# A fused encoder layer on one core: a reordered attention pipeline, more columns in the pair stage, and two half columns begun early

## The chip, the cores and the metric

The kernel runs on one core of one Trainium2 chip. The metric is the device time of one execution in microseconds, the median of several runs. A core has a matrix engine (PE, with its weight loads shown as PEld), a vector engine (DVE), a scalar engine (ACT), a general engine (POOL) and a queue engine (SP) that issues most transfers. Each engine works through its own instructions strictly in program order; semaphores tie the engines together.

## The reference

One layer of a streaming encoder, for 512 prompt tokens and 8 streams of 16 new tokens (640 rows together), with 2048 channels:

```
z = x @ w_in                  # q, k, v, forget and gate of attention; q, k, v, decay, beta and gate
                              # of the delta rule; two merge gates of 2048 columns each
A: 8 heads of forgetting attention (causal; the streams attend to 512 cached rows), * silu(gate) @ w_out_fox
B: 8 heads of the gated delta rule, convolution of width 4, in chunks,             * silu(gate) @ w_out_gdn
h  = (sigmoid(mA) * A + sigmoid(mB) * B) @ w_out
x1 = LayerNorm(2^0.25 * x + h)
y  = x1 + sigmoid(x1 @ w_pl_gate) * RMSNorm(p @ w_pl_proj)
```

Outputs are y, the new keys and values, log forgets, convolution tails and delta-rule states.

## The kernel before

**Columns and slots.** Activations lie transposed, 128 channels by 640 rows per tile. A *column* is 128 output channels. Every float32 operand is split into a high and a low part, and a product takes three matmuls. A *plain column* (`column`, with `mm6` at L396 and L397) has 16 *slots*; each does six matmuls of 320 rows, three for each half of the rows. A *pair* (`pair`, L474) computes two columns at once by a scheme of seven products of half size: 7 x 8 x 3 = 168 matmuls of 320 rows in place of 192. A *half pair* has half as many. The weights come as tiles of 1024 columns, and `w_piece` (L329, L332, L335, L342) splits them into pieces of 512: ACT copies the high part and DVE subtracts it for the low part; in the *accumulated* form ACT writes the negated high part and a transfer from POOL's queue adds the weights to it. A plain column takes 4 pieces, a pair 14 and four sums on DVE (`w_sum`, L319). At most five pieces are ahead. Some sums of weights are computed on POOL and kept in memory (`weight_sums`, L295).

**Stages.** First the *front*: two plain columns, four value columns (`wide`), then pairs: 8 for the gates, 2 for values, 11 for merge columns, 4 for queries and keys of the heads in `APART`. Then the *attention stage* (`phase_fox`): plain columns for the queries and keys of heads 1, 4 and 7, with three merge columns and the two columns of the embedding projection. Then the *delta-rule stage* (`phase_gdn`): three plain columns per head and as many merge columns behind head h as `FILL[h]` says; then two merge columns, `PLAIN` = 4 plain output columns of attention and four half pairs. Last the *tail*: the output columns of the delta rule, the pairs of w_out, and the gate.

**Order.** It is written out by a planner while the program is built. `tick` is called once per slot; each *lane* holds generators (attention, its decode part, outputs, convolution, block inverses, and so on) that issue some instructions and yield a number of slots to wait. The planner keeps a model of when each engine is done; a lane that yields a negative number goes on when the modelled finish less 1.5 us has come. The lanes on TensorE are looked at in every second slot (`every` = 2). `until` turns slots without dense matmuls until a condition holds; TensorE then has only what the lanes issue.

**Attention.** `fox_all` goes through 8 heads with four query blocks each. At each block `fox_step` moves a pipeline on: transposes of the block before last (L726), weights of the last one (`softmax2`, L655 and L656), the product with the values (L742) and the gate (L743); then `scores` of the new block (L388 to L390, L754, L759 to L650). `fox_dec` does the streams' part: scores against the cache (L773), softmax, and the product with cached values (L813). Cache tiles of the next head (4 of keys, 4 of values, 512 KB each) are loaded when those of this head are used. The first evacuation of the projection (`e_evac`) waits until the last decode is done.

**Delta rule.** Head by head a chain of generators: convolution, transposes and norms (`gdn`), block inverses (`gdn_blocks`, L1004 and L1006, 31 steps on DVE), merge, chunks, output (`gdn_out`, transposes at L1117). The half pairs need sums and splits of the attention outputs (`form_sums`, L1657; `form_splits`), and start only when head 7's inverses are done. The tail's first output column needs the last head's output in the last slot of each of its two groups.

Of the kernel before, what the change touches and what calls it, by code (L numbers as in the profile page):

```python
# [52 lines left out]
class Kernel:  # L53
# [19 lines left out]
    def __init__(self, tc, ins, outs):  # L73
        self.clock, self.busy, self.wrote, self.paced = 0.0, [0.0, 0.0, 0.0], {}, False
        self.tc, self.nc, self.i, self.o = tc, tc.nc, ins, outs
        self.lanes, self.every = [], 2
        self.banks, self.read, self.nbanks = [], {}, 3
        self.now = 0
# [119 lines left out]
    def plan(self):  # L198
# [55 lines left out]
        self.SUMMED = n - 48  # L254
# [144 lines left out]
    def column(self, cols=1, each=None, groups=((0, 16),), after=None, base=None, done=None):  # L399
# [7 lines left out]
        for n0, n1 in groups:  # L407
            ps = [tuple(self.gps(x.stop - x.start) for x in self.cut) for _ in range(cols)]
# [234 lines left out]
    def softmax1(self, xs, n):  # L643
# [3 lines left out]
        nm = self.zt([P, 1], "nm", 6)  # L647
        nc.vector.reduce_max(out=nm, in_=xs[:, 0:n], axis=AX.X, negate=True)
        sm = self.zt([P, 1], "sm", 6)
# [9 lines left out]
    def fox_in(self, h, q):  # L659

        nc = self.nc
        if h == 0:
            self.load_bias(0)
# [19 lines left out]

    def fox_all(self):


        flow = [None] * 4
        for h in range(H):
            while h not in self.heads or self.heads[h][2] > self.now or min(self.outdone, self.decdone) < h - 2:
                if any(flow):  # L690
                    self.fox_step(flow)
                yield 2
# [8 lines left out]
            for i in range(4):  # L701
                self.fox_step(flow)
                flow[0] = h, i, self.scores(h, i, q, k, parts)
# [14 lines left out]
    def fox_step(self, flow):  # L718

        nc = self.nc  # L720
        spread = weigh = None
        if flow[1]:
            h, i, (xs, _) = flow[1]
# [7 lines left out]
        if flow[0]:  # L731
            h, i, (xs, sm) = flow[0]
            self.softmax2(xs, P * (i + 1), sm)
            weigh = flow[0]
        if flow[2]:
            h, i, pT = flow[2]
            if i == 0:
                self.og = self.zt([P, T], "og", 2)
            vn, sl = self.vn[h], slice(i * P, (i + 1) * P)
            ops = self.sps()  # L740
            for kb in range(i + 1):
                nc.tensor.matmul(ops[:, 0:P], vn[:, kb, :], pT[:, kb * P:(kb + 1) * P], start=(kb == 0), stop=(kb == i))  # L742
            nc.vector.tensor_tensor(out=self.og[:, sl], in0=ops[:, 0:P], in1=self.sg[h][:, sl], op=ALU.mult)  # L743
            if i == 3:
                self.outs["gens"].append(self.fox_out(h, self.sg[h], self.og))
        flow[:] = None, weigh, spread, None

    def scores(self, h, i, q, k, parts):
# [9 lines left out]
        xs = self.zt([P, NPT], "xs", 3)  # L758
# [5 lines left out]
    def fox_dec(self, h, q, k):  # L764
# [12 lines left out]
        xd = self.zt([P, T], "xd")  # L777
# [12 lines left out]
        yield -2  # L790
        pt = self.dps()
# [10 lines left out]
        yield 4  # L802
# [418 lines left out]
    def run(self, ctx):  # L1221
# [18 lines left out]
        self.qkd = {(h, i): dr([P, T], F32, name=f"qkd{h}{i}") for h in (0, *self.APART) for i in range(2)}  # L1240
# [7 lines left out]
        self.outs, self.decs = self.lane(), self.lane()  # L1248
# [4 lines left out]
        with tc.manual_schedule():  # L1253
# [5 lines left out]
            with tc.tile_pool(name="ps2g", bufs=4, space=bass.MemoryType.PSUM) as self.ps2, \  # L1259
                    tc.tile_pool(name="cs2", bufs=1) as c2, tc.tile_pool(name="zg", bufs=1) as self.zp:  # L1260
                self.cvst = c2.tile([P, 24, 24], F32, name="cvst")
                nc.sync.dma_start(out=self.cvst, in_=self.i["conv"])
                self.nbanks = 4
                self.phase_gdn(conv, work)
            with tc.tile_pool(name="ps2b", bufs=4, space=bass.MemoryType.PSUM) as self.ps2, \
                    tc.tile_pool(name="zb", bufs=1) as self.zp:
                self.tail()
# [16 lines left out]
    def front(self, work):  # L1284
# [179 lines left out]
        def weights():  # L1464
# [3 lines left out]
            yield from self.weight_sums([t[:, x:x + 256] for t in ws for x in (0, 256)], slice(0, 12), (6, 4, 2))  # L1468
# [33 lines left out]
    def phase_fox(self, work):  # L1502
# [6 lines left out]
        self.heads, self.sg = {}, {}  # L1509
# [4 lines left out]
        ws = self.zt([P, 1024], "ws")  # L1514
        self.sums["gens"].append(self.weight_sums([ws[:, x:x + 256] for x in range(0, 1024, 256)], slice(12, 13),
                                                  (9, 7, 5, 20)))
        for h in range(H):
            qk = []
            if h in self.BETWEEN:
                self.mcol("eacc")  # L1520
            for c in range(2):
                stored = (h, c) in self.qkd
                if not stored:
                    acc = self.column()[0]
                self.until(lambda: min(self.qkdone) >= h - 2)
                x = self.zt([P, T], "qk"[c], 2)
                qk.append(x)
                if stored:
                    nc.sync.dma_start(out=x, in_=self.qkd[h, c])
                    continue  # L1530
                for hf in range(2):
                    sl = slice(hf * HALF, (hf + 1) * HALF)
                    if c == 0:
                        nc.scalar.mul(x[:, sl], acc[hf], FOX_SCALE)
                    else:
                        nc.scalar.copy(out=x[:, sl], in_=acc[hf])
                if c:
                    nc.sync.dma_start(out=self.o["fk"][h], in_=x)
            self.heads[h] = *qk, self.now + (9 if stored else 1)
        for _ in range(2 - len(self.BETWEEN)):  # L1540
            self.mcol("eacc")

        op, pr = [], []
        for k in range(2):
            if k == 0:
                self.until(lambda: not self.sums["gens"])
            pr.append(self.zt([P, 1024], "ws", 1, "pr")[:, 0:T] if k == 0 else self.zt([P, T], "pr"))
            nc.sync.dma_start(out=pr[k], in_=self.i["pT"][k])

        def after(s):  # L1550
            if s in (12, 14):
# [11 lines left out]
        nc.sync.dma_start(out=self.sqd, in_=self.eacc)  # L1563

# [10 lines left out]
    def phase_gdn(self, conv, work):  # L1575
# [76 lines left out]
        def form_sums(k, step):  # L1652

            a, b = fr[2 * k], fr[2 * k + 1]
            for o, x, y, op in ((b[:, xb], b[:, xb], a[:, xb], ALU.subtract), (a[:, xb], a[:, xb], a[:, xa], ALU.subtract),
                                (a[:, xa], b[:, xb], a[:, xa], ALU.add), (b[:, xa], b[:, xa], a[:, xa], ALU.subtract)):
                nc.vector.tensor_tensor(out=o, in0=x, in1=y, op=op)  # L1657
# [101 lines left out]
        store()  # L1759
        self.until(lambda: self.gdone == 7)  # L1760
# [15 lines left out]
    def e_evac(self, n, ps):  # L1776

        nc = self.nc
        if n == 0:
# [3 lines left out]
            tiles = [self.zt([P, 1024], *x, "e")[:, 0:T] for x in (("kc", 4), ("kc", 4), ("ws", 1), *[("vc", 4)] * 4)]  # L1783
# [59 lines left out]
    def tail(self):  # L1843
# [94 lines left out]
        for u in range(8):  # L1938
# [27 lines left out]
            self.column(groups=((0, 8), (8, 16)), base=8, each=each, after=after, done=gated)  # L1966
# [395 lines left out]
def _layout(a):  # L2362
# [21 lines left out]
    for h in range(1, H):  # L2384
        bl += [next(rest) for _ in range(h in Kernel.BETWEEN)]
        if h not in Kernel.APART:
            bl += [bq[h], bk[h]]
# [86 lines left out]
```

## Time and profile before

| | |
|---|---|
| median of 3 runs | 2173.64 us (2171.65 to 2174.12) |
| profiled execution | 2173.18 us |
| its span | 2171.3 us |
| PE, PEld, DVE, ACT, POOL busy | 2149.0, 2082.3, 1566.0, 1007.3, 401.9 us |
| transfers | 452.65 MB, 208 GB/s in the mean |
| front | 0 to 721.8 us |
| attention stage up to the projection | 721.8 to 941.2 us |
| last convolution column of head 7 done | 1432.8 us |
| half pairs | 1577.9 to 1636.4 us |

Busy time says how long an engine had work in it, not what it waited for. A matmul's record covers its way through the array, so that records overlap: the number of matmuls in a stretch tells their rate, and a stretch whose busy PE time is below its length has holes. The granted clock of TensorE is 0.999 of full speed in the mean.

### The profile page before, as it was taken

To read this page: it belongs to the slowest core of one execution; us is meant where nothing else is said; L and a number is where in the kernel's file an instruction comes from. 1 tells how busy PE (TensorE), PEld (TensorE's weight loads), DVE (VectorE), ACT (ScalarE), POOL (GpSimd) and SP (SyncE) were. 2 spreads that over 40 slices of the span, in tenths; PEclk is the share of its full clock that TensorE was granted. 3 is DMA by queue.
4 is the path that set the end of the run, shared out by engine and by line. 5 is a ranking of instruction groups with operands and counts; after the bars stand their busy time and mean duration, and the time that the engine had idled before them with its cause. 6 is when DMAs were issued, how large, how long until landed. Compare 5 with 4: busy or idle time off the path is not lost.

```text
span 2171.3 us, 41951 instructions
## 1 busy us (share of the span) xinstructions
PE 2149.0 (99%) x15438; PEld 2082.3 (96%) x15438; DVE 1566.0 (72%) x3207; ACT 1007.3 (46%) x2213; POOL 401.9 (19%) x596
## 2 busy tenths in 40 slices
PE   9999999999999999999999999999999999999998
PEld 7799999999999998899999999999999999999998
DVE  5877776767776565566478677766757787789987
ACT  4344443443444343353655566655443343354544
POOL 0022233323330101002334333332000000021100
PEclk9999999999999999999999999999999999999999
DMA  6356656666554899869978778878567656673465
GB/s 235 101 184 202 189 182 199 198 199 194 184 180 158 276 325 344 314 199 291 241 179 199 180 188 194 189 182 248 161 229 260 209 171 202 201 276 122 153 227 173
DMA packets 240670, 452.65 MB, mean 208 GB/s; under 512 B 38920, under 2 KB 122504, under 8 KB 240464
## 3 DMA queue, kind: packets, MB, share of 16 engines
q1 hardware_dynamic: 224912, 421.64, 59.5%
q0 software_dynamic: 15552, 28.32, 8.0%
q8 instruction: 122, 2.00, 0.4%
q14 instruction: 84, 0.69, 0.1%
HBM read 353.48 MB, written 96.38 MB: 207 GB/s over the span
## 4 chain that ended last, share of the span: by engine, by line
PE 91%; DVE 3%; DMA 3%; ACT 1%; SPq 0%; issue 0%; POOL 0%; ACTq 0%; DVEq 0%; POOLq 0%
PE g L474 44%; PE g L396 18%; PE g L397 18%; PE g L440 2%; PE s L974 1%; PE s L742 1%; PE s L813 1%; PE s L773 1%; DMA ws138b<-ws 0%; PE s L440 0%; PE s L1168 0%; DMA nb<-rd 0%; DVE sx L1006 0%; DVE sx L1004 0%; PE s L726 0%
## 5 line engine op out<-in xcount | busy, mean ns | idle before, releaser
L329 ACT CAST wh<-wr 128x512 fp32r<-128x512 f32 x624 | 381.2, 619 | 288.7 <-PE g L474 109.5
L335 DVE TENSOR_TENSOR wl<-wr,wh 128x512 fp32r<-128x512 f32 x516 | 358.3, 708 | 183.5 <-ACT wh L329 173.7
L474 PE MATMUL g<-xh,wh 128*128 128x320 f32 (+1 forms) x1296 | 402.9, 311 | 2.7 <-ACT m L1278 1.6
L474 PE MATMUL g<-xl,wh 128*128 128x320 f32 (+1 forms) x1296 | 401.2, 310 | 0.6 <-DVE xl L371 0.6
L474 PE MATMUL g<-xh,wl 128*128 128x320 f32 (+1 forms) x1296 | 401.4, 310 | 0.0
L396 PE MATMUL g<-xh,wh 128*128 128x320 f32 (+1 forms) x960 | 313.0, 326 | 0.7 <-ACT wh L329 0.7
L396 PE MATMUL g<-xh,wl 128*128 128x320 f32 (+1 forms) x960 | 297.1, 309 | 0.8 <-DMA wl<-in_w 0.7
L396 PE MATMUL g<-xl,wh 128*128 128x320 f32 (+1 forms) x960 | 297.2, 310 | 0.4 <-DVE xl L371 0.4
L397 PE MATMUL g<-xh,wh 128*128 128x320 f32 x960 | 297.3, 310 | 0.0
L397 PE MATMUL g<-xl,wh 128*128 128x320 f32 x960 | 297.0, 309 | 0.0
L397 PE MATMUL g<-xh,wl 128*128 128x320 f32 x960 | 296.7, 309 | 0.0
L474 PEld LDWEIGHTS g<-xh,wh 128*128 128x128 f32 x1296 | 243.9, 188 | 4.3 <-ACT m L1278 2.1
L474 PEld LDWEIGHTS g<-xl,wh 128*128 128x128 f32 x1296 | 243.7, 188 | 1.1 <-DVE xl L371 1.1
L474 PEld LDWEIGHTS g<-xh,wl 128*128 128x128 f32 x1296 | 244.1, 188 | 0.0
L474 PE MATMUL g<-t,wh 128*128 128x320 f32 (+1 forms) x1088 | 241.4, 310 | 0.0
L335 DVE TENSOR_TENSOR wl<-sr,wh 128x512 fp32r<-128x512 f32 x200 | 147.9, 759 | 98.6 <-ACT wh L329 97.6
L295 POOL TENSOR_TENSOR ws<-ws 128x171 f32<-128x171 f32 (+2 forms) x152 | 116.7, 768 | 541.5 <-DMA ws<-in_w 535.7
L396 PEld LDWEIGHTS g<-xh,wh 128*128 128x128 f32 x960 | 180.9, 188 | 11.9 <-issue 7.1
L474 PEld LDWEIGHTS g<-t,wh 128*128 128x128 f32 x1088 | 181.9, 188 | 0.6 <-issue 0.3
L396 PEld LDWEIGHTS g<-xh,wl 128*128 128x128 f32 x960 | 180.6, 188 | 1.4 <-DMA wl<-in_w 1.0
L397 PEld LDWEIGHTS g<-xh,wh 128*128 128x128 f32 x960 | 181.0, 189 | 0.9
L396 PEld LDWEIGHTS g<-xl,wh 128*128 128x128 f32 x960 | 180.9, 188 | 1.0 <-DVE xl L371 1.0
(440 smaller groups left out, 4148.8 us busy)
## 6 DMA issues: line engine op xcount, KB each, us to landing
wr<-in_w SPq DMA_DIRECT2D x252, 512.0 KB
wl<-in_w POOLq DMA_DIRECT2D x108, 256.0 KB, 5.8
kc<-in_kc SPq DMA_DIRECT2D x32, 512.0 KB
vc<-in_vc SPq DMA_DIRECT2D x32, 512.0 KB
sr<-in_w SPq DMA_DIRECT2D x25, 512.0 KB
ws<-in_w SPq DMA_DIRECT2D x96, 128.0 KB
sb<-in_w SPq DMA_DIRECT2D x80, 128.0 KB
md<-m SPq DMA_DIRECT2D x32, 320.0 KB
```

What stands on the lines that cost most here:

```text
L295: nc.gpsimd.tensor_tensor(out=o, in0=x, in1=y, op=op)
L329: nc.scalar.copy(out=hi, in_=src)
L335: nc.vector.tensor_tensor(out=lo, in0=src, in1=hi.bitcast(F32), op=ALU.subtract)
L396: nc.tensor.matmul(ps[0], whl[w], xhl[o][:, a], start=(first and x == 0), stop=(last and x == 2))
L397: nc.tensor.matmul(ps[1], whl[w], xhl[o][:, b], start=(first and x == 0), stop=(last and x == 2))
L440: nc.tensor.matmul(ps, x[:, sl], w, start=(s == 0 and n == 0), stop=(s == 15 and n == 2))
L474: nc.tensor.matmul(ps, a[:, w], b, start=(k == 0 and n == 0 and not more), stop=(k == last and n == 2), skip_group_check=True)
L742: nc.tensor.matmul(ops[:, 0:P], vn[:, kb, :], pT[:, kb * P:(kb + 1) * P], start=(kb == 0), stop=(kb == i))
L773: nc.tensor.matmul(s1[32 * j:32 * j + 32, :], self.qpad[:, 2 * j + par, :], kc[:, (j % 2) * NPT:(j % 2 + 1) * NPT], start=(par == 0), stop ...
L813: nc.tensor.matmul(od[32 * j:32 * j + 32, 0:P], self.ppad[:, c, 2 * j + par, :], vc[:, o:o + P], start=False, stop=(par == 1 and c == 3), ...
L974: nc.tensor.matmul(pp[:, o:o + 256].rearrange("p (a b) -> p a b", a=2), kq[:, 0, x], kq[:, :, x], start=True, stop=True)
```

## The change

In the front, one more pair of merge columns and one more pair of queries and keys: heads 1, 2, 3, 6 and 7 have them there, heads 4 and 5 in the attention stage. All heads' queries and keys go through memory and are loaded by `load_qk`. The attention stage has four query and key columns, three merge columns and the projection; its lanes are looked at in every slot and wait for the whole modelled finish. The list behind `fox_step` has five places instead of four; a block's weights, transposes and product with the values still come one, two and three steps after its scores, but the weights are now made after the new block's scores instead of before them; the decode part is cut in two generators in lanes of their own. Two merge columns fewer stand behind heads 6 and 7. The four form sums per block go from DVE to POOL, and the four plain output columns get their low parts in the accumulated form. One weight sum moves from the attention stage to the front. Before the wait for head 7's output the program issues seven of the eight slots of each half of the tail's first output column; the eighth follows in the tail. Weights and their order in memory are laid out accordingly.

```diff
-    FRONT = 32 - 3 - 7
-    APART = 2, 3, 5, 6
+    FRONT = 32 - 3 - 5
+    APART = 1, 2, 3, 6, 7
-    BETWEEN = 3, 6
-    FILL = 0, 0, 1, 0, 1, 0, 1, 4
+    JOBS = 4, 5, None, None
+    FILL = 0, 0, 1, 0, 1, 0, 0, 3
...
-        return abs(n), t + (0.25 if n > 0 else -1.5)
+        return abs(n), t + (0.25 if n > 0 else -self.lead)
...
-        self.SUMMED = n - 48
+        self.SUMMED = n - 44
...
+    def load_qk(self, h):
+        qk = []
+        for c in range(2):
+            qk.append(self.zt([P, T], "qk"[c], 2))
+            self.nc.sync.dma_start(out=qk[c], in_=self.qkd[h, c])
+        self.heads[h] = *qk, self.clock + (7 if h else 5)
...
-                    while self.qkdone[1] < h - 1:
+                    while self.qkdone[1] < h - 1 or h + 1 not in self.kept:
                         yield 1
                     self.load_bias(h + 1)
+                    if h:
+                        self.load_qk(h + 1)
...
     def fox_step(self, flow, new=None):
...
+        if flow[2]:
+            h, i, (xs, _) = flow[2]
...
+        if flow[3]:
+            h, i, pT = flow[3]
...
+        new = (*new[0:2], self.scores(*new)) if new else None
+        if flow[1]:
+            h, i, (xs, sm) = flow[1]
+            self.softmax2(xs, P * (i + 1), sm)
+        flow[:] = None, new, flow[1], spread, None
...
         self.softmax2(xd, T, sm)
         yield -2
+        self.decs2["gens"].append(self.fox_dec2(h, xd))
...
-        self.sums["gens"].append(self.weight_sums([ws[:, x:x + 256] for x in range(0, 1024, 256)], slice(12, 13),
-                                                  (9, 7, 5, 20)))
...
+        self.every, self.lead = 1, 0.0
...
+            nc.sync.dma_start(out=self.qkd[h, c], in_=x)
+            if c:
+                nc.sync.dma_start(out=self.o["fk"][h], in_=x)
+                self.kept.add(h)
...
         def after(s):
+            if s in (4, 6):
+                self.until(lambda: min(self.qkdone) >= 6)
...
-                nc.vector.tensor_tensor(out=o, in0=x, in1=y, op=op)
+                nc.gpsimd.tensor_tensor(out=o, in0=x, in1=y, op=op)
...
+        c, self.begun = self.col, []
+        for n in range(2):
+            ps = tuple(self.gps() for _ in range(2))
+            for s in range(8 * n, 8 * n + 7):
+                self.w_ahead()
+                self.mm6(ps, self.wk(c, s), nop[8 + s % 8], s % 8 == 0, False)
+                if s % 8 == 3:
+                    self.used += 1
+                self.tick()
+            self.begun.append(ps)
         self.until(lambda: self.gdone == 7)
         nop[15] = self.split(self.last)
...
+            if u == 0:
+                for n, ps in enumerate(self.begun):
+                    self.w_ahead()
+                    self.mm6(ps, self.wk(self.col, 8 * n + 7), self.op[15], False, True)
+                    self.used += 1
+                    each(8 * n)
+                    each(8 * n + 3)
+                    gated(ps)
+                self.col += 1
+                continue
```

More of the change, by code (lines that the diff above doesn't have):

```diff
@@ L1965, in after @@
                     next(last7)
-            self.column(groups=((0, 8), (8, 16)), base=8, each=each, after=after, done=gated)
+            if u == 0:
[8 more added lines that the diff above has]
+                continue
+            self.column(groups=((0, 8), (8, 16)), base=8, each=each, after=after, done=gated,
+                        banks=[self.sps() for _ in range(2)] if u == 1 else ())
         r = [None] * 16
@@ L2383, in _layout @@
     rest = iter(m[nf:nf + 3])
[L2384 to L2387, printed above, removed]
+    for h in Kernel.JOBS:
+        bl += [next(rest)] if h is None else [bq[h], bk[h]]
     bl += rest
```

128 lines of the change are left out of this document (56 added, 72 removed).

## The prediction

> **What bounds the kernel now.** I read the totals, then the chain that ended last, then tables of stretches cut at the stage boundaries, and last the waits of TensorE.
>
> ```profile
> span 2171.3 us, 41951 instructions
> ## 1 busy us (share of the span) xinstructions
> PE 2149.0 (99%) x15438; PEld 2082.3 (96%) x15438; DVE 1566.0 (72%) x3207; ACT 1007.3 (46%) x2213; POOL 401.9 (19%) x596
> ```
> ```profile
> PE 91%; DVE 3%; DMA 3%; ACT 1%; SPq 0%; issue 0%; POOL 0%; ACTq 0%; DVEq 0%; POOLq 0%
> ```
> TensorE is busy for 99% and carries 91% of the chain. Only two things can move the time: fewer or shorter matmuls, and TensorE's holes. The next table gives both; its columns are the stretch, its length, busy time (x instructions) of PE, PEld, DVE, ACT and POOL, granted clock, DMA share, GB/s.
>
> ```profile
> 162.80:217.10 54.30, 54.30 (x372) 54.30 (x371) 40.21 (x55) 22.93 (x41) 16.08 (x16) 1.00 0.63 203
> 651.40:705.70 54.30, 54.30 (x372) 54.30 (x371) 37.14 (x54) 22.37 (x41) 0.00 (x0) 1.00 0.47 158
> 721.80:941.20 219.40, 216.41 (x1949) 198.18 (x1949) 129.47 (x309) 84.69 (x224) 18.37 (x34) 1.00 0.86 306
> 970.00:1432.80 462.80, 460.99 (x3485) 444.07 (x3484) 321.43 (x995) 268.59 (x731) 164.77 (x280) 1.00 0.84 207
> 1432.80:1577.90 145.10, 142.47 (x1097) 136.14 (x1096) 100.74 (x299) 70.56 (x188) 25.84 (x48) 0.99 0.68 193
> 1577.90:1636.40 58.50, 57.86 (x424) 55.86 (x423) 37.06 (x83) 29.30 (x69) 0.61 (x1) 1.00 0.72 240
> 1636.40:2171.30 534.90, 526.26 (x3558) 523.85 (x3557) 435.08 (x754) 232.09 (x403) 28.99 (x64) 1.00 0.59 199
> ```
> The first row is the price: in the pair stage 372 matmuls of 320 columns start in 54.3 us, one per 0.146 us (a record lasts longer, since matmuls overlap). So a slot of six takes 0.876 us, a plain column of 96 takes 14.0 us, and a pair of columns by seven products (168) 24.5 us instead of 28.0. The attention stage (third row) has 3.0 us of TensorE holes, the delta-rule stage up to head 7's last column 1.8, the stretch after it 2.6, the half pairs 0.6. There is little to fill, so the gain must come from matmuls not issued.
>
> **The change part by part.**
>
> *Four plain columns become two pairs.* 2 x (192 - 168) = 48 matmuls fewer, 48 x 0.146 = **-7.0 us**. The pairs need more preparation: 14 pieces and 4 sums each, against 8 pieces for two plain columns.
>
> ```profile
> L335 DVE TENSOR_TENSOR wl<-wr,wh 128x512 fp32r<-128x512 f32 x516 | 358.3, 708 | 183.5 <-ACT wh L329 173.7 <-DMA wl<-in_w 4.2 <-DMA wr<-in_w 1.3
> L335 DVE TENSOR_TENSOR wl<-sr,wh 128x512 fp32r<-128x512 f32 x200 | 147.9, 759 | 98.6 <-ACT wh L329 97.6
> L319 DVE TENSOR_TENSOR sr<-wr,sr 128x1024 f32<-128x1024 f32 x50 | 66.6, 1331 | 3.1 <-DMA sr<-in_w 3.1
> ```
> 14 x 0.76 + 4 x 1.33 = 16 us of DVE per pair, under 24.5 us of matmuls; DVE is busy 37 to 40 us of 54.3 in pairs, so that costs nothing. Without this cover it would be 16 us a pair.
>
> *Weight sum 12 moves to the front.* POOL works there at 16 additions in 54.3 us and has finished by 651 (second row, 0.00), 70 us before the stage ends; the stage gets 49 us longer. One gate pair more is 16 additions and 32 SP transfers of 128 KB, about 54 us at that pace: nothing. If it were not covered, all of it would stand in front of the attention stage.
>
> *The attention stage has 7 plain columns instead of 9 before the embedding projection*: 112 slots, and 114 before the projection's first evacuation, which waits for the last decode head. The new pacing looks at its lanes in every slot instead of every second, but waits for the planner's full modelled finish instead of 1.5 us less. These counts are one of a slot's two halves, three matmuls each:
>
> ```profile
> 834.00:855.70 21.70, 12.38 (x42) 7.88 (x42) 1.00 1.02 380
> 855.70:879.40 23.70, 12.40 (x42) 7.90 (x42) 1.00 1.00 338
> 879.40:912.20 32.80, 17.68 (x60) 11.28 (x60) 1.00 0.85 304
> 912.20:941.10 28.90, 17.35 (x59) 11.16 (x60) 1.00 0.45 161
> ```
> ```profile
> L813 PE MATMUL s<-vc,ppad x512: 272/273/297, 771.2 to 931.3; 128*32 128x128 f32 x171
> ```
> ```profile
> L754 PE MATMUL s<-k,q x16: 272/275/377, 739.5 to 912.4; 128*128 128x128 f32 x16
> ```
> A head takes 42/3 = 14 slots, or 20 where it waits for its columns. The first scores come at 739.5, 17.7 us = 20 slots after the stage began; in the new code (5 us, then 9 yields) some 16. The last decode is done at 931.3, 19 us after head 7 starts, 12 of them slots. With s slots per head it fits if 16 + 7s + 12 <= 114, so s <= 12.3. How long a step must wait is DVE's work:
>
> ```profile
> L761 DVE TENSOR_TENSOR xs<-xs,cb 128x128 f32<-128x128 f32 x32 | 9.9, 308 | 1.1
> L681 DVE TENSOR_TENSOR kl<-k,kh 128x512 fp32r<-128x512 f32 x8 | 6.6, 820 | 0.0
> L759 DVE SCALAR_TENSOR_TENSOR xs<-nb,colT,s 128x512 f32<-128x512 f32 x8 | 5.9, 739 | 0.7 <-PE s L390 0.7
> L648 DVE TENSOR_REDUCE nm<-xs 128x1 f32<-128x512 f32 x8 | 5.5, 687 | 0.3
> ```
> The widest step is 0.74 + 0.31 + 0.69 and about 0.7 for weights and gate, some 2.6 us; the first, with its splits, some 3.5; the two between, scaled by their widths, 1.9 and 2.3: 10.3 us or 11.8 slots a head. Decode matmuls run inside these waits:
>
> ```profile
> 771.31 1.88 PE s L813 x64
> 776.36 1.85 PE s L773 x16
> ```
> 3.7 us a head in these rows of the chain in order of time, some 5 with their transposes. Decode's own DVE work lengthens the waits by some 3 us (an estimate: the same operations once more, on 640 columns), rounding adds half a slot per step: between 9 (all of decode's matmuls in the waits) and 14 (as now). I take 11, nearest the DVE sum: it fits, with 9 slots to spare. The pipeline is no deeper: a block still meets its weights one step, its transposes two and the values three steps after its scores. But its weights now stand behind the next scores on DVE, which gives the exponential a step's time, and the transposes behind a full wait for the weights. I let that halve the 3.0 us of holes: **-1.5 us**, bounds -3 (all) and 0 (new ones as large as the old). A throughput limit is not near: 129.5 us of DVE less 8 pieces in 191 us.
>
> *Queries and keys through memory.* Heads 1, 4 and 7 are loaded like the rest (6 loads more), and heads 4 and 5 stored first (4 stores). On SP's queue they stand behind waits for the column's ACT copy, with the cache loads behind them; those are issued a head early, so nothing. Saturation is a rival below.
>
> *Two fill columns fewer (28 us of cover) after heads 6 and 7, 84 matmuls (12.3 us) begun before head 7's output is needed.* The matmuls are only moved. Cover from head 7's last column to its output: 8 columns and 49.2 us of half pairs = 161 us before, 7 columns + 49.2 + 12.3 = 160 after. The chain it must hide:
>
> ```profile
> L1004 DVE TENSOR_TENSOR sx<-sx,lanes x248: 158/294/828, 1082.3 to 1554.6; 80x248 f32<-80x248 f32 x4, 80x232 f32<-80x232 f32 x4, 80x216 f32<-80x216 f32 x4, 80x200 f32<-80x200 f32 x4
> ```
> ```profile
> L1117 PE MATMUL s<-cb,ob x32: 270/272/273, 1211.8 to 1624.0; 128*128 128x128 f32 x32
> ```
> ```profile
> L1657 DVE TENSOR_TENSOR ogr<-ogr x16: 478/492/731, 1512.3 to 1557.5; 128x320 f32<-128x320 f32 x16
> ```
> The block inverses (31 steps, ended 1554.9) gate the half pairs, which start at 1577.9; the output transposes end at 1624.3, the half pairs at 1636.4. The half pairs come 28 us earlier. If head 7's chain moves only with its own columns (14 us), the inverses end at 1541 against 1550: no wait. If DVE's load holds it at today's absolute time, TensorE waits 5 us there and about 1 more at the end. I take **+0.5**, nearer the first, because DVE loses work in that stretch:
>
> ```profile
> L342 POOL DMA_DIRECT2D wl<-in_w x108 | 94.5, 881 | 200.9 <-ACT wl L332 162.9 <-ACT junk L935 12.6 <-ACT vn L1198 7.6
> L295 POOL TENSOR_TENSOR ws<-ws 128x171 f32<-128x171 f32 x80 | 54.6, 683 | 32.5 <-DMA ws<-in_w 28.3
> L295 POOL TENSOR_TENSOR ws<-ws 128x256 f32<-128x256 f32 x56 | 52.1, 930 | 507.0 <-DMA ws<-in_w 506.0
> ```
> *Form sums on POOL:* 16 x 0.49 us leave DVE; on POOL one takes about 930 x 320/256 = 1.2 us, 4.7 us a form instead of 2. *Accumulated low parts for four more columns:* 16 subtractions (16 x 0.71 = 11 us) leave DVE for ACT copies and 16 x 0.88 us of transfer issue on POOL. An issue can now stand behind four form sums (4.7 us) and its matmuls behind it; pieces are made some 14 us ahead, so nothing, bounds 0 and 4.7 per collision.
>
> *Tail.* The first half columns' last slots need the split of head 7's output at once instead of seven slots later; ACT and DVE (some 0.8 us each, as for L681) do it while the 84 matmuls run, if the output is done by then. DVE then waits for the first loads with the piece subtractions queued behind it, but three pieces (12 slots, 10.5 us) are ready. **+0.5**, bounds 0 and 2.
>
> Sum: -7.0 - 1.5 + 0.5 + 0.5 = **-7.5 us** on the profiled execution's 2173.2 us (span 2171.3 and 1.9 around it), which is 0.5 below the median of 2173.64 shown. From that median: **2166 us**.
>
> **The rivals.**
>
> *A, the transfers set the attention stage's pace.* Share and rate when they are full:
>
> ```profile
> 745.00:770.00 25.00, 24.41 (x174) 22.24 (x173) 16.69 (x41) 10.55 (x29) 3.42 (x6) 1.00 1.00 354
> 820.00:845.00 25.00, 25.00 (x281) 21.20 (x270) 11.76 (x29) 8.77 (x23) 2.72 (x7) 1.00 1.01 364
> 845.00:870.00 25.00, 23.73 (x220) 21.25 (x220) 16.84 (x39) 9.31 (x26) 4.10 (x6) 1.00 1.00 343
> 870.00:895.00 25.00, 24.98 (x231) 22.67 (x231) 16.05 (x43) 10.22 (x28) 0.47 (x2) 1.00 1.01 372
> 920.00:941.20 21.20, 20.39 (x197) 19.69 (x196) 11.56 (x27) 10.80 (x27) 0.00 (x0) 1.00 0.25 85
> ```
> Today 306 GB/s x 219.4 us = 67.1 MB, 1.8 of them in the last 21 us. Two weight columns (2.1 MB) and the weight sum (4.2) leave, 6 loads and 4 stores (3.3) come: 64.1 MB, 62.3 of them in the 170 us before the last decode. At the mean of the full rows, 358 GB/s, that takes 174 us: TensorE would wait 4 us, and the time would be 2170. Against it: cache rows are asked for a whole head ahead, and in two of the four full rows TensorE has no hole. The Trainium skill ("DMA: Bandwidth & Descriptors", section "Where 436 GB/s comes from") puts the limit per core between memory and SBUF at about 358 GB/s. By that rule this rival would be the forecast; the 372 of one row lies above it, so I do not take it as a wall.
>
> *B, slower: the attention lanes keep today's 14 slots per head.* Place: the waits in the last merge column and at the first projection evacuation. 16 + 98 + 12 = 126 slots against 114: 12 slots of TensorE standing still, 10.5 us, and the clock:
>
> ```profile
> 1446.00:1448.00 2.00, 0.52 (x4) 0.52 (x5) 1.90 (x5) 0.00 (x0) 0.00 (x0) 1.00 0.87 173
> 1448.00:1451.00 3.00, 3.00 (x13) 3.00 (x13) 2.90 (x8) 2.16 (x4) 0.17 (x1) 0.50 1.08 275
> ```
> After a hole of 1.5 us in a 2 us stretch the granted clock stood at 0.50 for some 3 us, costing 1.5 us. So -7.0 + 10.5 + two such drops (3) = +6.5: 2180. It decides from s = 13.5 on (8 slots, 7 us). For it: the finish is now waited for in full. Against it: today's even slots round up what a step needs. The Trainium skill ("TensorE: Matmul & The Clock Gate", section "Why this matters for your kernels") warns only of idle gaps above about 3 us. By that rule the shorter waits would leave the clock alone and B would be 2177; the two rows show a drop after less, so the trace decides.
>
> *C, the delta-rule chain stays where it is*: 6 us of waiting and a clock drop, 2173: the change does nothing in sum. For it: DVE was busy for 1.90 of 2.00 us where TensorE stood. Against it: the 19 us of work that leave DVE.
>
> **How the numbers follow.** Forecast 0.62, A 0.14, B 0.10, C 0.14. The forecast's own range is 2162 (all holes closed, nothing new: -10) to 2169. For eight in ten the range must take in A and C and leave B out: 2162 to 2174. A measurement of this kernel tells 0.2% (4.3 us) from no change. Faster by that means below 2169.3: the forecast nearly whole and a little under half of A, 0.67. Within it: the rest of A, C and a mild B, 0.22. Slower, above 2178: B and mishaps, 0.11.
>
> **What the profile after would show.** L474 with 336 more matmuls and L396/L397 with 384 fewer; the attention stage about 28 us shorter, with the same 3 us of holes or fewer; 33 instead of 42 matmuls of one line per head; no wait at the projection's first evacuation. Half pairs that follow the fourth plain column without a gap, and form sums on POOL at about 1.2 us. It would be wrong if TensorE waits for cache tiles or for the last decode near the stage's end (A, B), or for the inverses or POOL's accumulated pieces ahead of the half pairs (C), each with a clock below 1.0 behind it.

## The result, and the profile after

The changed kernel takes 2186.59 us in the median (2183.97 to 2191.57), the kernel before 2173.88 beside it. The ratio is 1.0062 with a 95% interval of 1.0048 to 1.0075: 13 us slower, where 7.5 faster had been forecast. The profiled execution has a span of 2187.1 us, 15.8 more than that of before.

The page of the changed kernel: span, busy times, and the chain that ended last.

```profile
span 2187.1 us, 41955 instructions
...
PE 2151.5 (98%) x15390; PEld 2077.5 (95%) x15390; DVE 1577.8 (72%) x3213; ACT 1021.2 (47%) x2234; POOL 426.3 (19%) x620
...
PE 87%; DMA 6%; DVE 3%; ACT 2%; issue 1%; SPq 1%; POOL 0%; ACTq 0%; DVEq 0%; POOLq 0%
```

48 matmuls are gone, as forecast, but transfers carry 6% of the chain instead of 3%. Stretches of the changed kernel (length; busy time and count of PE, PEld, DVE, ACT, POOL; granted clock, DMA share, GB/s): a pair, the attention stage from the front's end to the first convolution strip, the delta-rule stage, the plain columns, the half pairs, the rest; last the 168 us of the attention stage with most transfers.

```profile
162.80:217.10 54.30, 54.30 (x372) 54.30 (x371) 40.59 (x55) 22.36 (x40) 15.98 (x16) 1.00 0.62 198
771.10:1013.80 242.70, 230.55 (x1985) 205.66 (x1985) 145.62 (x341) 100.59 (x249) 7.13 (x23) 0.97 0.85 298
1013.80:1452.00 438.20, 436.47 (x3289) 420.56 (x3288) 311.61 (x953) 257.54 (x698) 159.27 (x267) 1.00 0.85 208
1452.00:1582.70 130.70, 128.37 (x1000) 121.67 (x999) 89.73 (x283) 72.32 (x191) 47.36 (x71) 1.00 0.87 232
1582.70:1652.00 69.30, 63.71 (x485) 60.13 (x485) 40.04 (x93) 33.82 (x88) 4.29 (x11) 0.98 0.62 214
1652.00:2187.10 535.10, 527.03 (x3563) 524.33 (x3562) 437.90 (x770) 233.91 (x409) 28.86 (x64) 0.99 0.59 199
...
785.00:953.00 168.00, 156.20 (x1419) 132.10 (x1418) 100.76 (x254) 64.63 (x176) 3.44 (x14) 0.96 0.95 335
```

The second of them in the kernel before:

```profile
721.60:975.10 253.50, 250.51 (x2179) 231.87 (x2178) 153.38 (x350) 105.09 (x262) 20.32 (x39) 1.00 0.85 299
```

The front grew by 49.3 us for two pairs, as costed. The attention stage has 194 matmuls fewer in the records, 28 us by their price, and is only 10.8 shorter: TensorE's holes went from 3.0 to 12.2 us and its clock to 0.97. The half pairs have 5.6 us of holes instead of 0.6. So -7.0 for matmuls, +9.2 and about +6 for holes and clock in the attention stage, +5.0 and about +1.5 in the half pairs: about 15, against 15.8 measured. (By lengths alone the attention stage lost 17 us and all that follows 5.) What TensorE waited for (total us, times, longest):

```profile
PE s L767 <- DMA k<-qkd: 4.3, 2, 2.4
PE s L786 <- DMA kc<-in_kc: 4.0, 1, 4.0
PE s L1205 <- DVE S L1221: 3.8, 1, 3.8
PE s L388 <- ACT pn L818: 3.8, 8, 1.3
PE s L1213 <- DVE uu L1091: 1.7, 1, 1.7
...
PE g L477 <- ACT t L1677: 1.6, 1, 1.6
```

Of these the kernel before had the one on DVE's `uu`, and single small ones on ACT's `pn`:

```profile
PE s L1196 <- DVE uu L1074: 1.9, 1, 1.9
...
PE s L388 <- ACT pn L801: 0.8, 1, 0.8
```

Two new ones end in transfers: first scores (L767) that wait for keys from memory, and the streams' scores (L786) that wait for cached keys. Both stand in the attention stage, with the clock behind them:

```profile
805.40:809.40 4.00, 0.10 (x1) 0.00 (x0) 2.58 (x7) 1.41 (x4) 0.00 (x0) 1.00 1.03 327
809.40:812.80 3.40, 3.28 (x10) 0.62 (x12) 0.11 (x1) 0.00 (x0) 0.00 (x0) 0.51 1.02 362
834.00:840.10 6.10, 4.21 (x82) 3.70 (x81) 1.46 (x6) 1.56 (x4) 0.41 (x2) 1.00 1.04 337
840.10:843.50 3.40, 3.40 (x20) 0.85 (x18) 2.33 (x6) 1.42 (x4) 0.00 (x0) 0.51 1.02 410
...
904.90:911.80 6.90, 6.28 (x26) 3.00 (x27) 3.54 (x9) 1.93 (x5) 0.24 (x2) 0.51 0.99 378
```

Why the cached keys are late shows in the rows of their tile: head 1's four loads after, then before.

```profile
L630 SPq DMA_DIRECT2D kc<-in_kc x4: 327/328/331, 798.4 to 802.2; - x4
...
DMA to landing us min/median/max: 11.1/11.1/11.1
```
```profile
L627 SPq DMA_DIRECT2D kc<-in_kc x4: 337/385/521, 751.0 to 752.5; - x4
...
L773 PE MATMUL s<-kc,qpad x16: 592/592/617, 776.3 to 777.6; 128*32 128x512 f32 x16
```

Before, they were asked for from 751.0 on and used at 776.3, 25 us later; the decode part of head 1 stood in one lane behind that of head 0. After, with the decode part cut in two lanes, they are asked for from 798.4 on and wanted at 805.4, 7 us later, while a load takes 11.1. A head's queries, asked for in the middle of the head before, take 9.7, where the planner counts 7; they are used 10 to 13 us after they are asked for. Before, it was 17 to 24 us. Head 2's after, then before:

```profile
L689 SPq DMA_DIRECT2D q<-qkd x1: 577/577/577, 828.6 to 828.6; - x1
...
DMA to landing us min/median/max: 9.7/9.7/9.7
```
```profile
759.02 0.37 SPq L1529 DMA_DIRECT2D q<-qkd  x1
...
781.00 0.39 PE L754 MATMUL s<-k,q 128*128 128x128 f32 x2
```

### The profile page after: what moved, and what is told of

Its sections match the earlier page's. It is cut to its first block, busy times and chain, and to the rows that moved or that the text cites. A ratio compares the mean times of both kernels' runs of the same rounds, so it can differ in the third digit from the quotient of the medians.

```text
span 2187.1 us, 41955 instructions
## 1 busy us (share of the span) xinstructions
PE 2151.5 (98%) x15390; PEld 2077.5 (95%) x15390; DVE 1577.8 (72%) x3213; ACT 1021.2 (47%) x2234; POOL 426.3 (19%) x620
## 4 chain that ended last, share of the span: by engine, by line
PE 87%; DMA 6%; DVE 3%; ACT 2%; issue 1%; SPq 1%; POOL 0%; ACTq 0%; DVEq 0%; POOLq 0%
PE g L477 45%; PE g L396 16%; PE g L397 16%; PE g L443 2%; DMA k<-qkd 1%; PE s L991 1%; PE s L786 1%; DMA kc<-in_kc 1%; PE s L748 1%; DVE sx L1023 1%; ACT wh L329 1%; DMA wr<-in_w 1%; PE s L830 1%; DVE sx L1021 1%; DMA ws138b<-ws 0%
## 5 line engine op out<-in xcount | busy, mean ns | idle before, releaser
L335 DVE TENSOR_TENSOR wl<-wr,wh 128x512 fp32r<-128x512 f32 x504 | 350.0, 709 | 164.1 <-ACT wh L329 160.6
L396 PE MATMUL g<-xh,wh 128*128 128x320 f32 (+1 forms) x888 | 291.0, 328 | 0.4 <-ACT wh L329 0.4
L396 PE MATMUL g<-xh,wl 128*128 128x320 f32 (+1 forms) x888 | 274.7, 309 | 0.9 <-DMA wl<-in_w 0.9
L396 PE MATMUL g<-xl,wh 128*128 128x320 f32 (+1 forms) x888 | 274.9, 310 | 0.4 <-DVE xl L371 0.3
L397 PE MATMUL g<-xh,wh 128*128 128x320 f32 x888 | 275.0, 310 | 0.0
L397 PE MATMUL g<-xl,wh 128*128 128x320 f32 x888 | 274.6, 309 | 0.0
L397 PE MATMUL g<-xh,wl 128*128 128x320 f32 x888 | 274.5, 309 | 0.0
L477 PEld LDWEIGHTS g<-xh,wh 128*128 128x128 f32 x1360 | 256.5, 189 | 3.9 <-ACT m L1294 2.1
L477 PEld LDWEIGHTS g<-xh,wl 128*128 128x128 f32 x1360 | 256.6, 189 | 0.0
L477 PE MATMUL g<-t,wh 128*128 128x320 f32 (+1 forms) x1120 | 248.6, 310 | 1.8 <-ACT t L1677 1.6
L335 DVE TENSOR_TENSOR wl<-sr,wh 128x512 fp32r<-128x512 f32 x216 | 159.3, 757 | 106.9 <-ACT wh L329 105.6
L329 ACT CAST wh<-sr 128x512 fp32r<-128x512 f32 x216 | 130.0, 618 | 141.2 <-PE g L477 110.4
L396 PEld LDWEIGHTS g<-xh,wh 128*128 128x128 f32 x888 | 167.5, 189 | 11.3 <-issue 7.6
L477 PE MATMUL g<-t,wl 128*128 128x320 f32 (+1 forms) x560 | 173.1, 309 | 0.0
L396 PEld LDWEIGHTS g<-xl,wh 128*128 128x128 f32 x888 | 167.3, 188 | 1.2 <-DVE xl L371 1.2
```

Of the source, the lines that this page charges most:

```text
L329: nc.scalar.copy(out=hi, in_=src)
L335: nc.vector.tensor_tensor(out=lo, in0=src, in1=hi.bitcast(F32), op=ALU.subtract)
L396: nc.tensor.matmul(ps[0], whl[w], xhl[o][:, a], start=(first and x == 0), stop=(last and x == 2))
L397: nc.tensor.matmul(ps[1], whl[w], xhl[o][:, b], start=(first and x == 0), stop=(last and x == 2))
L477: nc.tensor.matmul(ps, a[:, w], b, start=(k == 0 and n == 0 and not more), stop=(k == last and n == 2), skip_group_check=True)
```

## The experiments

Each run's ratio is to the kernel before on the same chip; in us it is the ratio less 1, times 2172, with an interval of 2 to 3 us to either side; a difference between two runs is less certain still. By this measure the changed kernel is at +13.5.

**The attention stage.** Three theories to begin with. W: loads are asked for too late, the rate is enough. B: the transfers' rate sets the pace (the prediction's rival A). P: the new pacing packs the steps too tightly.

*Planner told of longer loads:*

```
- self.heads[h] = *qk, self.clock + (7 if h else 5)
+ self.heads[h] = *qk, self.clock + (12 if h else 5)
# fox_dec, before the scores:
+ while h and self.clock < self.keys[h]: yield 1    # 14 us after the key loads
```


> Only the planner's times for two kinds of loads are changed: a head starts 12 us instead of 7 after its queries and keys are asked for, and the decode scores of a head wait until 14 us after its cache keys were asked for. Theory W (loads are asked for too late, the rate is enough): the waits for queries, keys and cache keys (8.7 us) and the three half-clock stretches behind them (13.6 us long, 6.8 lost) go; about -12 to -15 us, 2172 to 2175. Theory B (the transfers at full rate set the stage's pace): the waits turn into slots without columns or move to the next load; within 3 us of 2186.6. Theory P (the new pacing packs the steps too tightly): a part of the gain, as the pacing itself stays, some -5 us.

1.0144 (1.0131 to 1.0157), +31.3. The waits for loads are gone, and yet it is 18 us slower: heads 3 to 7 start 24 to 25 us behind the one before, the columns run out, and a whole head runs bare. A stretch without dense matmuls, and the longest wait of the stage:

```profile
919.10:947.30 28.20, 18.86 (x151) 13.51 (x150) 17.08 (x48) 10.00 (x30) 0.42 (x2) 0.81 0.90 315
```
```profile
PE s L738 <- DVE xs L659: 7.6, 6, 2.6
```

W in this form falls: where every head waits longer, the heads' own sequence no longer fits into the columns. (Which of the two longer waits does it is not told apart here.) Theory H takes its place: what a head needs must be asked for earlier.

*One decode lane:* `self.decs2["gens"].append(self.fox_dec2(h, xd))` becomes `yield from self.fox_dec2(h, xd)`.


> The decode part is one generator in one lane again, so a head's decode scores stand behind the last head's product with the cached values. Theory W: the 4.0 us wait for cache keys at 805 and the half clock behind it (1.7 us) go, the waits for queries and keys stay; -5 to -6 us, about 2181. Theory B: no change beyond 2 us, since the bytes are the same. Theory P: no change beyond 2 us.

1.0097 (1.0084 to 1.0110), +21.1; a miss for all three. The cached keys are in time: head 1's scores come at 815.6, 16 us after the loads are asked for. So the cut in two lanes makes up about 9 of the 18 us by which that distance shrank. But queries and keys now cost four times as much, since the code asks for them only when the last head's decode scores are out, and those come later in one lane:

```profile
PE s L767 <- DMA k<-qkd: 17.8, 6, 5.0
```

*Old pacing:* `self.every, self.lead = 2, 1.5` in the stage.


> The attention stage's lanes are looked at in every second slot and wait for the modelled finish less 1.5 us, as before the change. Theory P: heads take 14 slots again, loads are ready, and the holes of the stage go from 12 us to some 4, with slots without columns at its end: between -8 and 0 us. Theory W: steps are issued earlier against their data but heads further apart: the waits for loads shrink by half, -4 us, and up to 5 us of empty slots come at the end; within 3 us of 2186.6. Theory B: as W, no change.

1.0093 (1.0080 to 1.0106), +20.2, outside all three forecasts. P falls: the new pacing is worth some 7 us here.

*Queries and keys asked for one block earlier:*

```
- if i == 1 and h + 1 < H: ... if h: self.load_qk(h + 1)
+ if i == 0 and 0 < h < H - 1: ... self.load_qk(h + 1)
```


> The queries and keys of head h+1 are asked for behind the first block of head h instead of the second; nothing waits longer. Theory H (the heads' own sequence sets the stage, and what a head needs must be asked for earlier, since waiting longer only moves the heads apart): the waits for queries and keys (4.3 us) and the two half-clock stretches behind them (10.2 us, 5.1 lost) go, the one for cache keys at 805 stays; -6 to -9 us, 2178 to 2181. Theory B (the rate of the transfers): the wait comes back at cache keys or values, within 3 us of 2186.6.

1.0043 (1.0030 to 1.0055), +9.3: 4 us, less than H said and more than B said. The waits for queries and keys are gone; the one for cached keys stands:

```profile
PE s L788 <- DMA kc<-in_kc: 3.7, 1, 3.7
```

*The same, and head 1's decode scores wait for the planner's 14 us:* `while h == 1 and self.clock < self.keys[h]: yield 1`.


> As the run with earlier queries and keys, and the decode scores of head 1 alone wait until 14 us after its cache keys were asked for. Theory H: the 4.0 us wait at 805 and its half clock (1.7) go too; -10 to -14 us, 2173 to 2177. Theory B: within 3 us of 2186.6.

1.0005 (0.9997 to 1.0014), +1.1: 12 us of the 13.5 are back. The stage, its 168 us of heavy transfers, and the fullest stretch in them:

```profile
771.00:996.90 225.90, 221.90 (x1987) 204.02 (x1986) 144.98 (x342) 100.19 (x250) 6.75 (x23) 1.00 0.87 318
785.00:953.00 168.00, 164.01 (x1582) 146.68 (x1585) 110.92 (x282) 70.78 (x194) 2.96 (x14) 1.00 0.96 356
835.00:860.00 25.00, 25.00 (x238) 21.91 (x231) 17.20 (x44) 10.36 (x28) 0.42 (x2) 1.00 1.01 389
```

225.9 us is the old stage's 253.5 less the 28 of its missing matmuls, with holes of 4.0 us. 356 GB/s went through in the same 168 us in which the changed kernel moved 335, and in 25 us of full transfers TensorE had no hole. H holds and B falls. The rate was there to be had; the time between a request and its use was too short. Asking earlier mended that for queries and keys. For head 1's cached keys it was waiting longer, which cost nothing that shows in this place.

*Value cache loaded once:* `load_kv` returns head 0's tile for the values of heads 1 to 7.


> The changed kernel as it is, but the cached values of head 0 are used for all heads, which leaves out 28 loads of 512 KB (14.7 MB of some 63 in the stage) and so computes another result. Rival A (the transfers' rate sets the stage's pace): all waits of the stage go, -14 us, 2172. Theory H (single loads are asked for too late): the keys of head 1 still come late, the queries and keys come sooner behind a shorter queue; -4 to -7 us, 2180 to 2183.

1.0040 (1.0027 to 1.0053), +8.7. A quarter of the stage's bytes less brings 5 us, as much as asking earlier for queries and keys. The cached keys are as late as ever, at a mean rate of 265 GB/s:

```profile
PE s L789 <- DMA kc<-in_kc: 3.9, 1, 3.9
```
```profile
785.00:953.00 168.00, 159.91 (x1479) 138.61 (x1478) 107.39 (x274) 68.21 (x186) 3.09 (x14) 0.98 0.78 265
```

**The pairs, the form sums, the low parts, the begun columns.** Theory D: head 7's chain lost its cover behind heads 6 and 7, and waits eat a part of the pairs' 7 us.

*The pairs alone, in the kernel before:* `FRONT = 24`, `APART = 2, 3, 5, 6, 7`, `FILL = 0, 0, 1, 0, 1, 0, 0, 3`.


> The kernel before with nothing but the two pairs: merge columns and the queries and keys of one more head (2, 3, 5, 6, 7) in the front, two columns fewer in the attention stage, two fewer behind heads 6 and 7; old pipeline, pacing, forms and tail. If the pairs are worth their 48 matmuls wherever they stand: 2166 to 2168. Theory H: 12 slots per head are asked of a stage that takes 14: some 10 us of slots without columns and clock drops, 2174 to 2180, and theory D adds up to 6 us.

1.0179 (1.0166 to 1.0192), +38.9. That is far above both forecasts. An old head keeps its 14 slots (42 matmuls of L396), and then the columns are out; the stage takes 246.1 us instead of the 225.5 that 28 us of matmuls fewer would leave. Head 1, and a stretch bare of dense matmuls:

```profile
807.20:829.90 22.70, 12.55 (x42) 7.89 (x42) 1.00 0.92 332
```
```profile
902.30:939.70 37.40, 27.81 (x256) 18.49 (x255) 20.86 (x53) 12.32 (x37) 4.38 (x8) 0.82 1.00 355
```

The other 25 us are lost behind it. This kernel has neither the low parts from POOL's queue nor the begun columns, which the runs below price at 16 and 6; that these make up the 25 is argued from those prices, not shown.

*Form sums back on DVE:* `nc.gpsimd.tensor_tensor` becomes `nc.vector.tensor_tensor`.


> The 16 form sums go back from POOL to DVE; nothing else. If the forms on POOL are what makes the half pairs wait (form splits end at 1587 while the half pairs start at 1583; 1.8 us of waiting there), 2 to 4 us are gained: 2183 to 2185. If the last head's chain on DVE sets that stretch (the 4.0 us wait for the state at 1610 with a half clock behind it), 16 sums more on DVE delay it: no gain or up to 4 us slower. The attention stage is the same in all theories.

1.0048 (1.0034 to 1.0063), +10.4. With the mended loads the same step gives 2.6 (below). Either difference lies within the intervals; both say about 3. The first theory had the size, but its wait does not go: the half pairs wait for a split form for 2.7 us with the sums on DVE and for 1.6 with them on POOL. What goes is the 3.8 us wait for the state. On POOL the 16 sums take 0.88 us each, and the last ends at 1584.0, behind the start of the half pairs at 1582.7:

```profile
L1666 POOL TENSOR_TENSOR ogr<-ogr x16: 857/876/1207, 1541.0 to 1583.1; 128x320 f32<-128x320 f32 x16
```

A copy of head 7's chain (`uu`, L1050) stands behind it in POOL's order and starts at 1584.0; with the sums on DVE it starts at 1566.3. That this is how the state came late is likely, not shown.

*Loads and forms mended:* queries and keys asked for one block earlier and head 1's 14 us, as above, with the forms on DVE.


> The run with earlier queries and keys and head 1's key wait (2172.5), and with the form sums on DVE. Theory H: the attention stage is then as long as its matmuls, and what is left of the loss is the end of the delta rule, where the holes of the profile with forms on DVE were 4.6 us smaller than with forms on POOL; 2167 to 2169. If that difference was chance (its two medians overlap): 2172.

0.9993 (0.9984 to 1.0002), -1.5, or 2170.3 in the median, between the two forecasts.

*The fill columns back, in the changed kernel:* `FRONT = 22`, `FILL = 0, 0, 1, 0, 1, 0, 1, 4`.


> The pair of merge columns of the front goes back to two plain columns behind heads 6 and 7; the rest of the change stays. 24 matmuls more are 3.5 us. Theory D (the delta-rule chain lost its cover: 1.8 + 1.8 + 4.0 us of waits and 1.7 of half clock between 1550 and 1618): these waits go, -4 to -6 us net, 2181 to 2183. If the waits there have another cause (form sums on POOL, the plain columns' pieces): 2190.

1.0103 (1.0090 to 1.0116), +22.4: 9 us slower, where 24 matmuls are 3.5. D missed here. Other waits came in its place, for columns' evacuations:

```profile
PE g L477 <- DVE fx L486: 4.0, 2, 2.4
PE g L396 <- ACT fx L1720: 3.0, 1, 3.0
```

*The same with loads and forms mended:*


> As the run with loads and forms mended, but the pair of merge columns goes back to two plain columns behind heads 6 and 7; the pair of queries and keys stays. Theory D: the 3.5 us of 24 matmuls are paid and some 4 us of waits go, 2169 to 2171. If only the matmuls count: 2174. With forms on POOL this step was 8 us slower; if that is what happens here too, 2178.

1.0003 (0.9995 to 1.0012), +0.7, so 2.2 slower than with the pair, between the two forecasts and within the intervals: most of the matmuls, little of D. The 9 us above need the form sums on POOL or the late loads; which of them, and how, stays open.

*Both pairs undone, loads and forms mended:* `FRONT = 22`, `APART = 1, 2, 3, 6`, `JOBS = 4, 5, 7, None, None`, the old `FILL`.


> As the run with loads and forms mended, but without the two pairs: merge columns and head 7's queries and keys are plain columns in the stages again, 48 matmuls more. If a pair is worth its 24 matmuls once loads are in time: 7 us slower than that run. If the two columns more in the attention stage, or behind heads 6 and 7, hide waits that are still there: 0 to 4 us slower.

1.0005 (0.9996 to 1.0014), +1.1: the pairs are worth 2.6 of their 7.0, which the intervals tell from 7 but not from nothing. The half pairs are where the rest goes, without pairs and then with them:

```profile
1580.70:1638.80 58.10, 56.86 (x415) 54.83 (x415) 36.98 (x83) 29.00 (x68) 0.61 (x1) 1.00 0.67 236
```
```profile
1563.90:1633.50 69.60, 64.64 (x488) 60.35 (x487) 41.44 (x96) 32.91 (x86) 0.61 (x1) 0.98 0.63 219
```

Holes of 5.0 us instead of 1.2, and a clock of 0.98. 73 more matmuls of the lanes stand among them, head 7's chain, which without the pairs ran beside plain columns. The largest wait, though, is not for that chain but for the split of a form sum of the attention outputs:

```profile
PE g L477 <- ACT t L1682: 2.7, 1, 2.7
```

ACT starts the last of these splits at 1569.4, 5.5 us after the half pairs begin. Without the pairs it starts it at 1556.6, 24 us ahead of them. So what is missing is time for both, the delta-rule chain and the forms.

*Nothing begun, loads and forms mended:* `self.begun = []`, and the tail's first column as the others.


> As the run with loads and forms mended, but the 84 matmuls of the tail's first column stand in the tail again. The prediction's reason for them: they cover 12.3 us of head 7's chain, whose last transposes come some 6 us after the half pairs, so 6 to 10 us slower with a half clock. Rival: the chain is done by then anyway once its sums are on DVE: within 1 us.

1.0021 (1.0011 to 1.0030), +4.6: 6 slower than with them, as expected. The wait is for head 7's output, with 6.8 us of half clock behind it:

```profile
PE s L1139 <- ACT ob L1134: 3.4, 1, 3.4
```

*Old low parts, loads and forms mended:* `self.SUMMED = n - 48`.


> As the run with loads and forms mended, but the low parts of the four plain output columns are subtracted on DVE again, 16 subtractions of 0.71 us, in place of ACT copies and transfers from POOL's queue. The prediction's reason (DVE sets head 7's chain): up to 4 us slower. Rival: no change beyond 1.5 us, since the transfers from POOL wait for ACT as long.

1.0068 (1.0055 to 1.0081), +14.8: 16 slower, a miss for both. The plain columns behind head 7's last column, with old and then with new low parts:

```profile
1437.30:1575.10 137.80, 129.68 (x996) 122.47 (x994) 101.19 (x313) 66.87 (x181) 22.15 (x40) 0.97 0.64 186
```
```profile
1435.70:1563.90 128.20, 127.96 (x998) 121.32 (x997) 89.58 (x294) 71.97 (x191) 37.91 (x64) 1.00 0.87 231
```

11.6 us of DVE more, as counted, and for as many matmuls 8.1 us of holes in place of 0.2. This stretch is 9.6 of the 16 us; 4.4 more show in the tail. The longest wait is for the block inverses on DVE, at most 0.2 with the new low parts:

```profile
PE s L1218 <- DVE sx L1026: 5.4, 1, 5.4
```

*One fill column moved from head 4 to head 7:* `FILL = 0, 0, 1, 0, 0, 0, 0, 4`, loads and forms mended.


> As the run with loads and forms mended, but one fill column moves from behind head 4 to behind head 7; the same matmuls. Theory D (of the pairs' 7 us some 4 are eaten, because head 7's chain lost a column of cover): 2 to 4 us faster, 2166 to 2168. If the cover isn't what costs them: 2170, within 1 us.

0.9982 (0.9972 to 0.9993), -3.9: 2168.44 us in the median, the fastest of all, and faster than the kernel before. The half pairs have 1.1 us of holes and the full clock:

```profile
1566.90:1629.00 62.10, 60.97 (x478) 57.47 (x477) 38.69 (x89) 31.30 (x76) 0.84 (x1) 1.00 0.64 225
```

The wait for a split form is gone. That speaks for D, in the wider sense of cover for the chain and the forms, though the step from -1.5 to -3.9 alone lies within both intervals.

*The last middle column moved too:* `FILL = 0, 0, 0, 0, 0, 0, 0, 5`.


> As the run before, with the last middle fill column moved too, so that all five stand behind head 7. Theory D: as that run or up to 1 us better, unless the middle heads wait for their chunks without the columns, then 1 to 5 us worse than it. Without theory D: 2170 or worse.

1.0008 (0.9999 to 1.0016), +1.7. The time alone does not decide, since both forecasts reach it. The end is as good, but two half-clock stretches of 6.8 us appear in the middle heads, at 1270 and 1390, where that column had stood.

## Why the prediction was wrong, step by step

- **The step that failed** is "those are issued a head early, so nothing", on queries, keys and cache loads: put at 0, it measured +12.4 us (from +13.5 to +1.1 when queries and keys are asked for a block earlier and head 1's cached keys are used later). I counted bytes and queue places, and not the time between a request and its use, though this change altered both ends: for head 1's cached keys it went from 25 to 7 us, about 9 of those 18 by the cut decode part, and `load_qk` stands in the middle of the head before, 10 to 13 us ahead of the use. Half of the rows for it stand in the trace of before: when the next head's loads were issued and used. That trace gives no landing time for a load of 512 KB; the nearest is 5.8 us in the median for the 256 KB transfers from POOL's queue, already close to the 7 us that were left.
- **-7.0 for the pairs**: price and count were right (49.3 us in the front, 48 matmuls fewer), but with the loads and forms mended they net 2.6, which may be nothing. **+0.5 for the delta rule** was the term that was too small; about 4 belong there. That is only in part rival C's mechanism: the wait is in the half pairs rather than at the inverses, and 2.7 us of it are for the split of a form sum, which the prediction gave no time.
- **-1.5 for holes in the attention stage** did not come. Mended, it has 4.0 us of them on 225.9, against 3.0 before.
- **11 slots a head**: nearly. In the mended run heads 4 to 7 start 19.9 to 21.0 us behind the one before, with 30 to 36 matmuls of one line, 10 to 12 slots; the first heads took 12 to 15. The mean is 12.0, just under the 12.3 that fit. The projection's first evacuation has no wait.
- **The weight sum in the front at nothing**: nothing shows against it; the front has its length.
- **Form sums on POOL** were over-costed per piece (0.88 us, not 1.2) and under-costed in place: about 3 us, which shows in the wait for the delta-rule state.
- **Low parts** were put at nothing. With the two pairs in, they carry the end of the delta rule: without them it is 16 us slower. (The kernel before did without them, and had the cover of two more columns there.) "DVE loses work in that stretch" was the right thought, and worth far more than I gave it.
- **Tail +0.5**: without the begun columns it is 6 us slower, so they do cover the end of head 7's chain; what the term itself measures was not told apart.
- **Rival A** had the place (the attention stage), but not the mechanism: at 389 GB/s over 25 us nothing waits. The Trainium skill ("DMA: Bandwidth & Descriptors", section "Where 436 GB/s comes from") puts the limit per core between memory and SBUF at about 358 GB/s. The 389 is above it, and the measurement decides. **Rival B** did not come, but the pairs alone show that it was real: with the old pipeline the stage loses 21 us to bare slots and the clock behind them.

By ratios, taken in this order, the parts add up: pairs -2.6, late loads +12.4, form sums +2.6, all the rest +1.1 (not to be told from 0), 13.5 together.

## What to carry to other kernels

When a change reorders a pipeline, list for every load when it is asked for and when it is used, before and after, and compare that with issue-to-landing times under the load of that stage; bytes per second say nothing about it. A planner that gives a load a fixed time needs the time that the load takes there, and where the sequence itself has to fit under other work, a late load is mended by asking earlier; waiting longer helps only where that sequence has time to spare, as at head 1's cached keys. Edits that share an engine's slack (here DVE behind the last head) cannot be costed one by one at nothing.

## What the runs showed of the hardware

The same hole can cost a half clock or not. The changed kernel at 834 to 840.1 and the run with forms on DVE, whose attention stage is the same program, have nearly the same stretch there; one then runs at 0.51 and the other at 1.00. The second:

```profile
834.00:840.00 6.00, 4.09 (x83) 3.51 (x78) 1.35 (x6) 1.27 (x4) 0.41 (x2) 1.00 1.03 347
840.00:843.50 3.50, 3.50 (x30) 2.06 (x23) 3.04 (x8) 1.42 (x4) 0.00 (x0) 1.00 1.02 410
```

Half-clock stretches come in pieces of 3.4 us: many of 3.4, some of 6.8, and one of 13.7 in each of the runs with the pairs alone and with the old low parts. The Trainium skill ("TensorE: Matmul & The Clock Gate", section "Why this matters for your kernels") warns of idle gaps above about 3 us. Here a stretch with under 2 us idle in 6 brought the drop, though not each time. That may be why the changed kernel's runs spread over 7.6 us; it was not tested apart. And a load of 512 KB of cached keys took 9 to 11 us from issue to landing while the DMA share was about 1.0, which no mean rate shows.
